# Attention output split over ten steps from step 48, and four rows of the output projection as filler

## The chip, the cores and the metric

The kernel runs on one core of a Trainium2 chip. The metric is the time of one execution on the device in microseconds; the kernel before took 1182.82 us (median of three runs, 1179.34 to 1183.29).

## The reference

A decoder trunk of two layers on one sequence of 1024 tokens with 1024 channels, in float32. The change is in the second layer only: forgetting attention with 16 heads of 64 channels, a gate, and the output projection.

```python
o = lax.map(one_block, (qb, fq, jnp.arange(nblk)))        # softmax(q k + forget bias) v, 8 blocks of 128 queries
o = o.transpose(1, 0, 3, 2, 4).reshape(bsz, L, ATTN_WIDTH)
o = o * jax.nn.silu(z.astype(jnp.float32))                # o_t in the kernel
return o.astype(h.dtype) @ w_out                          # rows f of the kernel
# and then x = x + gate * y
```

## The kernel before

All activations lie transposed: channels on the 128 partitions, tokens along the free side. A matrix of 1024 channels is eight tiles k = 0 to 7 of 128 x 1024, and most work goes by half of the tokens, i = 0 and 1 (512 each). A product in float32 is made from parts: `split` (line 100) writes a high part on ACT (L94) and the rest, x minus high part, on DVE (L102) or, for some weights, on POOL; `project_part` (L113) then issues three matmuls of 128 x 128 by 512 for each k. One half of a row of the output projection is thus 24 matmuls into one PSUM tile.

The attention runs as a list of 64 steps: heads 0 to 15, and for each head four blocks c = 0 to 3 of 256 queries, with 2c + 2 key blocks in block c. Step j first issues the scores of step j + 2 (`scores`: matmuls `sp`, DVE minimum `pr`/`mx`, ACT exponent, DVE reciprocal `sm`, POOL scaling of `pr`), then its own `values`: PE transposes `tp`, their split on ACT (`pth`) and DVE (`ptl`), matmuls `ov`, an ACT copy `ob` and a DVE sum `oc`. After each odd head (h = 1) and each odd block, POOL multiplies half i of tile p of `o_t` (which holds the gated z of two heads) by `oc` (L1301); this half is then done. For p = 6 and 7 it is split at once.

Filler is a generator from which the loop takes parts, each of three matmuls: two per step up to step 59, four from step 60 on, and all that is left behind step 63 (`some_fill`). A part is queued behind the last `ov` of its step on PE. First it gives the z projection (`zb`, eight strips of 16 parts); by the count of calls the last part of z on half 0 is given at step 47, the last on half 1 at step 51. Then comes `first_rows`. Before the change it makes tiles `aH`, `aL` for both halves, and begins rows of the output projection: row 0 over k = 0 to 5 for half 0, then half 1, each parked (evacuated with the residual into a tile `xr`); then rows 1 and 2 on half 0 over all k, and the rest of row 0 on half 0. The splits of the twelve halves of `o_t` that are done by then (`todo`) are asked for by this generator: three before its first part, one before each of the next nine. Where a part needs a half that isn't done, the call returns with nothing.

Behind the loop, the rest: row 1 on half 1 (in a PSUM bank of its own, around the wait for the last split), the rest of row 0, and rows 2 to 7, each half a tile `pj_f`, evacuated by DVE (`xr`, L1224) and stored.

The weights of a row come by one load into `w_raw` (a single buffer) and a split into `w_hi`, `w_lo` (two buffers each); row 2's go into a buffer `wf` that held the keys of head 14. The order of instructions on each engine is set by a planner at build time, from the order of the program, the dependences, its own estimate of durations, and the `issue_after` blocks, which put an instruction behind another one on its engine. Each engine, and each queue of loads, then runs in that order. PSUM tiles of z, of the rows f and of `ov` share two banks (`pj`).

Of the kernel before, what the change touches and what calls it, by code (L numbers as in the profile page):

```python
# [12 lines left out]
F32 = mybir.dt.float32  # L13
F32R = mybir.dt.float32r
# [6 lines left out]
P = 128  # L21
D = 1024
KT = D // P
# [8 lines left out]
HL = L // 2  # L32
# [2 lines left out]
MAGIC = 12582912.0  # L35
LOOK = 2
U_FIRST = 4
F_ROWS, Z_END = 3, 4
Z_FIRST, Z_STEP = 8, 2
ORDER = ((0, 0), (0, 1), (0, 2), (0, 3), (1, 0), (1, 1), (1, 2), (1, 3))  # L40
OUT_SEQ = ((0, 0), (1, 0), (0, 1), (1, 1), (2, 0), (2, 1), (3, 0), (3, 1),
# [4 lines left out]
def trunk(tc, a, out):  # L46
# [3 lines left out]
    with top:  # L50
# [24 lines left out]
        vec, at0 = {}, 0  # L75
# [29 lines left out]
        def act_tiles(more=0, halves=(0, 1)):  # L105
            return [[[apool.tile([P, HL + more * i], F32R, name=f"a{p}{k}_{i}", tag=f"a{p}{k}_{i}") if i in halves else None
                      for i in range(2)] for k in range(KT)] for p in "HL"]


        def project_part(ps, w, act, half, ks, k0=0, k1=KT - 1):  # L110
            for k in ks:
                for n, (wt, at) in enumerate(((0, 0), (0, 1), (1, 0))):
                    m = T.matmul(ps, w[wt][:, k, :], act[at][k][half], start=(k == k0 and n == 0), stop=(k == k1 and n == 2)).ins  # L113
            return m
# [91 lines left out]
        with l0:  # L206
# [141 lines left out]
            for k in (4, 5, 6, 7, 0, 1, 2, 3):  # L348
                pool, tag = ((s5, "ut"), (s5, "bbs"), (s5, "x1m"), (s5, "x2m"))[k - 4] if k >= 4 else (xp, "xw")
# [63 lines left out]
            for c in range(2):  # L413
                ps, m = chunk(w2, c, "u2")
# [377 lines left out]
            for k in range(KT):  # L792
                pool, tag = ((s5, "bb"), (s5, "bbs"), (s5, "x1m"), (s5, "x2m"), (sbm, "min_"), (s5, "ut"), (sb, "uu"), (sb, "uu"))[k]
# [22 lines left out]
        with l0b:  # L816
# [8 lines left out]
            for e, i in [(e, i) for e in range(KT - 2) for i in range(2)] + [(e, i) for i in range(2) for e in (KT - 2, KT - 1)]:  # L825
# [18 lines left out]
                if e:  # L844
                    ps = project(wg[e], act, i, f"g{e}_{i}", psa, "psa")
                    S.activation(sg, ps, AF.Sigmoid, bias=vec["b_glu"][:, e:e + 1])
                V.tensor_tensor(out=zs, in0=sg, in1=zs, op=ALU.mult)
                gated = V.tensor_tensor(out=part(yt[e], i), in0=part(yt[e], i), in1=jk(zs), op=ALU.mult).ins
# [7 lines left out]
            psb = top.enter_context(tc.tile_pool(name="psb", bufs=3, space=PSUM, side="right", reuse_waits="tile"))  # L856
            gate_a = mod_bias(16, 24, "gate_a")
            held, acc, seen, pending = {}, [None] * 2, [0, 0], None
            for e, i in OUT_SEQ:
# [6 lines left out]
                xr = wk.tile([P, HL], F32, name="xr", tag="zt2")  # L866
                xd = Q.dma_start(out=xr, in_=a["xT"][:, e, sl]).ins
                mod_load(xd)
                ps = project(held[e][1], act, i, f"o{e}_{i}", psa, "psa", pending)
# [35 lines left out]
        with l1a:  # L905
# [127 lines left out]
            for j, job in enumerate(("v0", "v2", "k0", "k2", "q0", "q2")):  # L1033
# [19 lines left out]
                for i in range(2):  # L1053
                    if job == "k2" and i:
                        act_b = act_tiles(0, (0,))
                    elif job == "q0" and i:
                        lx.close()
                        modx.close()
                        at0 = top.enter_context(tc.tile_pool(name="at0", bufs=2, side="right", reuse_waits="tile"))
# [150 lines left out]
            return scores(hds[n], c)  # L1210


        wf, parked, act2, done = {}, {}, [], set((k, 0) for k in range(KT - 2))

        def split_o(k, i):
            split(o_t[k][:, HL * i:HL * i + HL], act2[0][k][i], act2[1][k][i])

        def residual(e, i, park=False):
            xr = at_.tile([P, HL], F32, name="xr2", tag="park" if park else "oc", bufs=2 if park else 3)
            Q.dma_start(out=xr, in_=x1_d[P * e:P * e + P, HL * i:HL * i + HL])  # L1220
            return xr

        def gated(ps, e, xr):
            V.scalar_tensor_tensor(out=xr, in0=ps, scalar=gate_b[:, e:e + 1], in1=xr, op0=ALU.mult, op1=ALU.add)  # L1224

        def final(ps, e, i):
            xr = parked.pop((e, i)) if (e, i) in parked else residual(e, i)
            gated(ps, e, xr)
            Q.dma_start(out=out[P * e:P * e + P, HL * i:HL * i + HL], in_=xr)

        def f_tile(e, i, pool=None):
            return (pool or pj).tile([P, HL], F32, name=f"f{e}_{i}", tag="psb" if pool else "pj")

        def wf_(e):
            if e == 2 and e not in wf:

                w = at0.tile([P, 2, KT, P], F32R, name="wf2", tag="kk")
                raw = wpool.tile([P, KT, P], F32, name="w_raw", tag="w_raw", bufs=1)
                Q.dma_start(out=raw, in_=a["b_w_out"][e])
                wf[e] = w[:, 0], w[:, 1]  # L1240
                split(raw, *wf[e])
            elif e not in wf:
                wf[e] = weight_strip(a["b_w_out"][e], [P, KT, P], G if e < 2 else V)
            return wf[e]

        def first_rows():
            act2.extend(act_tiles())
            wf_(0), wf_(1)
            todo = [(k, i) for i in range(2) for k in range(KT - 2)]
            for i in range(2):  # L1250
                ps = f_tile(0, i)
                for k in range(KT - 2):
                    for _ in range(3 if (k, i) == (0, 0) else 1):
                        if todo:
                            with tc.issue_after(ends[-1][1]), tc.issue_after(ends[-1][2]):
                                split_o(*todo.pop(0))
                    project_part(ps, wf_(0), act2, i, (k,), 0, KT - 3)
                    yield
                parked[0, i] = residual(0, i, True)
                gated(ps, 0, parked[0, i])  # L1260
            wf_(2)
            for e in range(1, F_ROWS):
                ps = f_tile(e, 0)
                for k in range(KT):
                    while (k, 0) not in done:
                        yield
                    project_part(ps, wf_(e), act2, 0, (k,))
                    yield
                final(ps, e, 0)
                if e == 1:  # L1270
                    ps = f_tile(0, 0)
                    for k in (KT - 2, KT - 1):
                        project_part(ps, wf_(0), act2, 0, (k,), KT - 2)
                        yield
                    final(ps, 0, 0)

        fill = itertools.chain(z_fill, first_rows())

# [9 lines left out]
        ends = []  # L1288
        for j, (n, c) in enumerate(steps):
            if j + LOOK < len(steps):  # L1290
                pend.append(ahead(j + LOOK))
            if j < 2:
                with tc.issue_after(sp_end[-1]):
                    some_fill(3)
            ends.append(values(n, hds[n], c, pend.pop(0)))
            with tc.issue_after(ends[j][0]):
                some_fill(Z_STEP if j < 60 else Z_END)
            p, h = n // 2, n % 2
            if h and c % 2:
                sl = slice(HL * (c // 2), HL * (c // 2) + HL)  # L1300
                G.tensor_tensor(out=o_t[p][:, sl], in0=o_t[p][:, sl], in1=ocs.pop((p, c // 2)), op=ALU.mult)  # L1301
                done.add((p, c // 2))
                if p >= KT - 2:
                    split_o(p, c // 2)
        some_fill(999)

        psl = f_tile(1, 1, psb)
        project_part(psl, wf_(1), act2, 1, range(KT - 1))
        ps = f_tile(0, 1)
        project_part(ps, wf_(0), act2, 1, (KT - 2, KT - 1), KT - 2)  # L1310
        final(ps, 0, 1)
        project_part(psl, wf_(1), act2, 1, (KT - 1,))
        final(psl, 1, 1)
        for e in range(2, KT):
            for i in range(int(e < F_ROWS), 2):
                final(project(wf_(e), act2, i, f"f{e}_{i}"), e, i)

# [51 lines left out]
```

## Time and profile before

| | |
|---|---|
| median of three runs | 1182.82 us (1179.34 to 1183.29) |
| the profiled execution | 1183.26 us, of which the span from the first to the last instruction is 1181.1 us |
| PE busy | 97% of the span |
| DVE busy | 71% |
| ACT busy | 51% |
| POOL busy | 30% |
| mean granted clock of PE | 0.994 |

Times in views of the trace count from the span's start. A busy PE is not PE at its peak, since matmuls are pipelined and their ends modelled: matmuls of 512 columns issue every 0.23 us, and each record is some 0.4 us long, so records overlap. In the same way two DVE records in a row overlap a little at their edges. Idle time of an engine is put down to the semaphore that came last. A few matmul records are missing from the trace.

### The profile page before, as it was taken

To read this page: it belongs to the slowest core of one execution; us is meant where nothing else is said; L and a number is where in the kernel's file an instruction comes from. 1 tells how busy PE (TensorE), PEld (TensorE's weight loads), DVE (VectorE), ACT (ScalarE), POOL (GpSimd) and SP (SyncE) were. 2 spreads that over 40 slices of the span, in tenths; PEclk is the share of its full clock that TensorE was granted. 3 is DMA by queue.
4 is the path that set the end of the run, shared out by engine and by line. 5 is a ranking of instruction groups with operands and counts; after the bars stand their busy time and mean duration, and the time that the engine had idled before them with its cause. 6 is when DMAs were issued, how large, how long until landed. Compare 5 with 4: busy or idle time off the path is not lost.

```text
span 1181.1 us, 20618 instructions
## 1 busy us (share of the span) xinstructions
PE 1146.0 (97%) x7506; PEld 1018.0 (86%) x7506; DVE 838.3 (71%) x1721; ACT 605.6 (51%) x1141; POOL 349.8 (30%) x572
## 2 busy tenths in 40 slices
PE   8999999988999999999999999999999999989998
PEld 7688888887888887999999999988988889877786
DVE  6768999875788975836867654358888887897421
ACT  6665777565534333423222533247777777785210
POOL 2300122112000152211343354435545454544100
PEclk9999999999999999999999999999999999999999
DMA  9664567686875873258953438236647464541242
GB/s 360 205 182 141 150 171 178 151 198 180 316 248 188 291 277 99 81 195 261 309 177 108 167 102 251 90 109 143 133 102 161 105 147 102 132 90 45 98 162 71
DMA packets 94661, 197.11 MB, mean 167 GB/s; under 512 B 17728, under 2 KB 42496, under 8 KB 93024
## 3 DMA queue, kind: packets, MB, share of 16 engines
q1 hardware_dynamic: 86768, 174.17, 49.6%
q0 software_dynamic: 6048, 16.85, 4.7%
q10 hardware_dynamic: 1744, 4.77, 1.8%
q8 instruction: 59, 0.97, 0.3%
q14 instruction: 42, 0.34, 0.1%
HBM read 138.21 MB, written 46.27 MB: 156 GB/s over the span
## 4 chain that ended last, share of the span: by engine, by line
PE 73%; DVE 9%; ACT 7%; DMA 6%; issue 3%; POOL 1%; SPq 0%; ACTq 0%; DVEq 0%
PE tkps L940 22%; PE pj_g L113 8%; PE pj_o L113 7%; PE zb L113 6%; PE pj_f L113 5%; PE u L265 5%; PE tp L1184 4%; PE ov L1190 3%; DMA v<-v 3%; PE ov L1191 2%; PE sp L1151 2%; PE sp L1152 2%; PE f L113 2%; ACT pr L1159 1%; ACT w_hi L94 1%
## 5 line engine op out<-in xcount | busy, mean ns | idle before, releaser
L940 PE MATMUL tkps<-wvh,aH 128*128 128x256 f32 (+1 forms) x768 | 220.2, 287 | 3.3 <-DVE hnt L969 3.3
L940 PE MATMUL tkps<-wvl,aH 128*128 128x256 f32 (+1 forms) x768 | 216.6, 282 | 0.0
L940 PE MATMUL tkps<-wvh,aL 128*128 128x256 f32 (+1 forms) x768 | 216.0, 282 | 0.0
L940 PEld LDWEIGHTS tkps<-wvh,aH 128*128 128x128 f32 x768 | 145.2, 189 | 4.1 <-DVE hnt L969 3.7
L940 PEld LDWEIGHTS tkps<-wvl,aH 128*128 128x128 f32 x768 | 145.5, 189 | 0.3 <-issue 0.2
L940 PEld LDWEIGHTS tkps<-wvh,aL 128*128 128x128 f32 x768 | 144.8, 189 | 0.5 <-issue 0.5
L1161 POOL TENSOR_SCALAR pr<-pr,sm 128x128 f32<-128x128 f32 (+7 forms) x128 | 97.0, 763 | 98.5 <-DVE sm L1160 98.4
L1186 ACT ACTIVATE pth<-tp 128x512 fp32r<-128x512 f32 (+1 forms) x192 | 86.9, 489 | 57.0 <-PE ov L1190 30.8
L1159 ACT ACTIVATE pr<-pr,mx 128x128 f32<-128x128 f32 (+7 forms) x128 | 98.9, 773 | 27.1 <-DVE mx L1156 26.1
L1187 DVE TENSOR_TENSOR ptl<-tp,pth 128x512 fp32r<-128x512 f32 (+1 forms) x192 | 101.3, 552 | 11.2 <-ACT pth L1186 9.7
L1156 DVE CUSTOM_DVE_ANT_0 pr<-sp,msk 128x512 f32<-128x512 f32 (+3 forms) x128 | 72.8, 570 | 28.0 <-PE tp L1184 22.1
L713 POOL DMA_DIRECT2D y_d<-r x64 | 33.4, 552 | 200.2 <-ACT r L708 199.1
L94 ACT ACTIVATE w_hi<-w_raw 128x1024 fp32r<-128x1024 f32 x48 | 50.7, 1055 | 72.9 <-PE pj_f L113 28.1
L1184 PE MATMUL tp<-ident,pr 128*128 128x128 f32 x576 | 83.1, 273 | 3.0 <-DVE ptl L1187 2.7
L1190 PE MATMUL ov<-pth,vhl 128*128 128x256 f32 x320 | 84.5, 297 | 0.6 <-ACT pr L1159 0.4
L964 ACT ACTIVATE hsq<-tkps 128x256 f32<-128x256 f32 x64 | 24.3, 384 | 114.6 <-PE tkps L940 109.5
L1184 PEld LDWEIGHTS tp<-ident,pr 128*128 128x128 f32 x576 | 68.6, 140 | 13.8 <-DVE ptl L1187 4.7
L1191 PE MATMUL ov<-ptl,vhl 128*128 128x256 f32 x320 | 80.1, 284 | 0.0
L1151 PE MATMUL sp<-kk,qs 128*128 128x256 f32 (+2 forms) x192 | 70.1, 368 | 3.9 <-DVE mx L1156 3.9
L967 POOL TENSOR_TENSOR hms<-hms,nhalf 128x4 f32<-128x4 f32 x64 | 70.8, 1106 | 5.3
L1152 PE MATMUL sp<-kk,q 66*128 66x256 f32 (+2 forms) x192 | 65.6, 345 | 0.0
L265 PE MATMUL z<-aH,w_hi 128*128 128x258 f32 (+2 forms) x192 | 62.7, 327 | 1.4 <-ACT ez L405 1.4
(346 smaller groups left out, 3154.6 us busy)
## 6 DMA issues: line engine op xcount, KB each, us to landing
modw<-modw SPq DMA_DIRECT2D x48, 512.0 KB
wvr<-kvq_w SPq DMA_DIRECT2D x12, 1024.0 KB
w_raw<-a_w_in SPq DMA_DIRECT2D x16, 512.0 KB
v_d<-vt POOLq DMA_DIRECT2D x32, 256.0 KB, 4.3
kk<-k_d SPq DMA_DIRECT2D x16, 512.0 KB
vhl<-v_d SPq DMA_DIRECT2D x16, 512.0 KB
qs<-q_d SPq DMA_DIRECT2D x32, 256.0 KB
w_raw<-a_w_out SPq DMA_DIRECT2D x10, 512.0 KB
```

Source lines behind the costliest of these rows:

```text
L113: m = T.matmul(ps, w[wt][:, k, :], act[at][k][half], start=(k == k0 and n == 0), stop=(k == k1 and n == 2)).ins
L265: m = T.matmul(ps[:, 0:c1 - c0], w[wt][:, k, :], act[at][k][i][:, c0:c1], start=(k == 0 and n == 0), stop=(k == KT - 1 and n == 2)).ins
L940: T.matmul(ps[:, 0:nv], at, wt[:, k, 0:nv], start=(n == 0), stop=(n == 3 * KT - 1))
L1151: T.matmul(sp[:, 0:wm_], qsl, kk[:, 0, lo:lo + wm_], start=True, stop=False)
L1152: sp_end.append(T.matmul(sp[:, 0:wm_], q1_[:, P * i:P * i + P], kk[0:HD + 2, 1, lo:lo + wm_], start=False, stop=True).ins)
L1159: S.activation(pr[:, 0:nk], pr[:, 0:nk], AF.Exp, scale=-1.0, bias=mx, accum_out=sm)
L1161: G.tensor_scalar(out=pr[:, 0:nk], in0=pr[:, 0:nk], scalar1=sm, scalar2=0.0, op0=ALU.mult, op1=ALU.add)
L1184: T.transpose(out=tp[:, b, :], in_=prs[qi][:, P * (b0 + b):P * (b0 + b) + P], identity=ident)
L1186: S.activation(pth[:, 0:m, dst], tp[:, 0:m, :], AF.Copy)
L1187: V.tensor_tensor(out=ptl[:, 0:m, dst], in0=tp[:, 0:m, :], in1=pth[:, 0:m, dst].bitcast(F32), op=ALU.subtract)
L1190: T.matmul(ov, vhl[:, b, :], pth[:, b - b0, :], start=(b == 0), stop=False)
L1191: end = T.matmul(ov, vhl[:, b, :], ptl[:, b - b0, :], start=False, stop=(b == nb - 1)).ins
```

## The change

The twelve splits are no longer asked for by the filler. The loop itself asks for them behind `values` of its step, by a table: 2, 1, 2, 1 at steps 48 to 51 (half 0 of tiles 0 to 5) and one at each of steps 52 to 57 (half 1). The tiles `aH`, `aL` are made for half 0 at step 48 and for half 1 at step 52. The splits stay tied behind `ob` on ACT and `oc` on DVE of their step.

`first_rows` now parks rows 0 and 1, each in both halves, over k = 0 to 5 (four parked tiles, 24 parts); then it makes the rest (k = 6, 7) of rows 0 and 1 on half 0, and then rows 2 and 3 on half 0 over all k: 44 parts in all, 30 before. Row 2's weights are asked for behind the third parked half row, row 3's behind the end of row 1 on half 0, into buffers that held head 14's queries. Behind the loop, the half row that is spread around the last split is row 2's, and rows 0 and 1 are both ended there on half 1.

```diff
--- before.py
+++ after.py
@@ -35,7 +35,8 @@
 MAGIC = 12582912.0
 LOOK = 2
 U_FIRST = 4
-F_ROWS, Z_END = 3, 4
+F_ROWS, Z_END = 4, 4
+SPLIT_AT = {48: 2, 49: 1, 50: 2, 51: 1, 52: 1, 53: 1, 54: 1, 55: 1, 56: 1, 57: 1}
 Z_FIRST, Z_STEP = 8, 2
 ORDER = ((0, 0), (0, 1), (0, 2), (0, 3), (1, 0), (1, 1), (1, 2), (1, 3))
 OUT_SEQ = ((0, 0), (1, 0), (0, 1), (1, 1), (2, 0), (2, 1), (3, 0), (3, 1),
@@ -1210,13 +1211,15 @@
             return scores(hds[n], c)
 
 
-        wf, parked, act2, done = {}, {}, [], set((k, 0) for k in range(KT - 2))
+        wf, parked, done = {}, {}, set((k, 0) for k in range(KT - 2))
+        act2 = [[[None] * 2 for _ in range(KT)] for _ in range(2)]
+        todo = [(k, i) for i in range(2) for k in range(KT - 2)]
 
         def split_o(k, i):
             split(o_t[k][:, HL * i:HL * i + HL], act2[0][k][i], act2[1][k][i])
 
         def residual(e, i, park=False):
-            xr = at_.tile([P, HL], F32, name="xr2", tag="park" if park else "oc", bufs=2 if park else 3)
+            xr = at_.tile([P, HL], F32, name="xr2", tag="park" if park else "oc", bufs=4 if park else 3)
             Q.dma_start(out=xr, in_=x1_d[P * e:P * e + P, HL * i:HL * i + HL])
             return xr
 
@@ -1232,47 +1235,43 @@
             return (pool or pj).tile([P, HL], F32, name=f"f{e}_{i}", tag="psb" if pool else "pj")
 
         def wf_(e):
-            if e == 2 and e not in wf:
-
-                w = at0.tile([P, 2, KT, P], F32R, name="wf2", tag="kk")
+            if e in (2, 3) and e not in wf:
+
+                if e == 2:
+                    w = at0.tile([P, 2, KT, P], F32R, name="wf2", tag="kk")
+                    wf[e] = w[:, 0], w[:, 1]
+                else:
+                    wf[e] = at0.tile([P, KT, P], F32R, name="wf3h", tag="qs"), at0.tile([P, KT, P], F32R, name="wf3l", tag="q1_0", bufs=1)
                 raw = wpool.tile([P, KT, P], F32, name="w_raw", tag="w_raw", bufs=1)
                 Q.dma_start(out=raw, in_=a["b_w_out"][e])
-                wf[e] = w[:, 0], w[:, 1]
                 split(raw, *wf[e])
             elif e not in wf:
                 wf[e] = weight_strip(a["b_w_out"][e], [P, KT, P], G if e < 2 else V)
             return wf[e]
 
+
+
         def first_rows():
-            act2.extend(act_tiles())
             wf_(0), wf_(1)
-            todo = [(k, i) for i in range(2) for k in range(KT - 2)]
-            for i in range(2):
-                ps = f_tile(0, i)
+            for e, i in ((0, 0), (1, 0), (0, 1), (1, 1)):
+                ps = f_tile(e, i)
                 for k in range(KT - 2):
-                    for _ in range(3 if (k, i) == (0, 0) else 1):
-                        if todo:
-                            with tc.issue_after(ends[-1][1]), tc.issue_after(ends[-1][2]):
-                                split_o(*todo.pop(0))
-                    project_part(ps, wf_(0), act2, i, (k,), 0, KT - 3)
+                    project_part(ps, wf_(e), act2, i, (k,), 0, KT - 3)
                     yield
-                parked[0, i] = residual(0, i, True)
-                gated(ps, 0, parked[0, i])
-            wf_(2)
-            for e in range(1, F_ROWS):
-                ps = f_tile(e, 0)
-                for k in range(KT):
+                parked[e, i] = residual(e, i, True)
+                gated(ps, e, parked[e, i])
+                if (e, i) == (0, 1):
+                    wf_(2)
+            for e in range(F_ROWS):
+                ps, k0 = f_tile(e, 0), 0 if e > 1 else KT - 2
+                for k in range(k0, KT):
                     while (k, 0) not in done:
                         yield
-                    project_part(ps, wf_(e), act2, 0, (k,))
+                    project_part(ps, wf_(e), act2, 0, (k,), k0)
                     yield
                 final(ps, e, 0)
                 if e == 1:
-                    ps = f_tile(0, 0)
-                    for k in (KT - 2, KT - 1):
-                        project_part(ps, wf_(0), act2, 0, (k,), KT - 2)
-                        yield
-                    final(ps, 0, 0)
+                    wf_(3)
 
         fill = itertools.chain(z_fill, first_rows())
 
@@ -1293,6 +1292,14 @@
                 with tc.issue_after(sp_end[-1]):
                     some_fill(3)
             ends.append(values(n, hds[n], c, pend.pop(0)))
+            for _ in range(SPLIT_AT.get(j, 0)):
+                k, i = todo.pop(0)
+                if k == 0:
+                    for p_, x in enumerate(act_tiles(0, (i,))):
+                        for kk_ in range(KT):
+                            act2[p_][kk_][i] = x[kk_][i]
+                with tc.issue_after(ends[-1][1]), tc.issue_after(ends[-1][2]):
+                    split_o(k, i)
             with tc.issue_after(ends[j][0]):
                 some_fill(Z_STEP if j < 60 else Z_END)
             p, h = n // 2, n % 2
@@ -1304,14 +1311,16 @@
                     split_o(p, c // 2)
         some_fill(999)
 
-        psl = f_tile(1, 1, psb)
-        project_part(psl, wf_(1), act2, 1, range(KT - 1))
-        ps = f_tile(0, 1)
-        project_part(ps, wf_(0), act2, 1, (KT - 2, KT - 1), KT - 2)
-        final(ps, 0, 1)
-        project_part(psl, wf_(1), act2, 1, (KT - 1,))
-        final(psl, 1, 1)
-        for e in range(2, KT):
+
+        psl = f_tile(2, 1, psb)
+        project_part(psl, wf_(2), act2, 1, range(KT - 1))
+        for e in range(2):
+            ps = f_tile(e, 1)
+            project_part(ps, wf_(e), act2, 1, (KT - 2, KT - 1), KT - 2)
+            final(ps, e, 1)
+        project_part(psl, wf_(2), act2, 1, (KT - 1,))
+        final(psl, 2, 1)
+        for e in range(3, KT):
             for i in range(int(e < F_ROWS), 2):
                 final(project(wf_(e), act2, i, f"f{e}_{i}"), e, i)
 
```

## Rows read from the trace of the kernel before

**Rows 1.** The page of the profile: busy time of each engine (first part), and the shares of the chain that ended last, by engine (fourth part).

```profile
PE 1146.0 (97%) x7506; PEld 1018.0 (86%) x7506; DVE 838.3 (71%) x1721; ACT 605.6 (51%) x1141; POOL 349.8 (30%) x572
...
PE 73%; DVE 9%; ACT 7%; DMA 6%; issue 3%; POOL 1%; SPq 0%; ACTq 0%; DVEq 0%
```

**Rows 2.** Busy time of each engine in windows of four steps, each from the last `oc` of one head to the last `oc` of the next: steps 44 to 47, then S1 to S4. Columns: window, its length, busy us of each engine (instructions), granted clock of PE, share of the DMA engines, GB/s.

```profile
1003.68:1022.70 19.02, 18.83 (x123) 16.63 (x123) 15.79 (x49) 14.37 (x34) 10.61 (x19) 1.00 0.59 137
1022.70:1041.68 18.98, 18.98 (x129) 17.25 (x128) 15.16 (x50) 13.94 (x35) 8.82 (x18) 1.00 0.56 113
1041.68:1067.58 25.90, 21.03 (x120) 16.84 (x120) 23.96 (x62) 20.52 (x47) 12.32 (x17) 0.96 0.39 92
1067.58:1091.65 24.07, 24.03 (x141) 20.61 (x141) 17.60 (x49) 15.08 (x33) 9.02 (x20) 0.97 0.11 34
1091.65:1109.23 17.58, 15.96 (x102) 13.10 (x101) 9.40 (x18) 6.81 (x15) 2.93 (x6) 1.00 0.15 53
```

**Rows 3.** The same view in windows of 5 us, from the middle of S2 to the start of S3.

```profile
1050.00:1055.00 5.00, 5.00 (x33) 4.36 (x32) 4.94 (x13) 3.26 (x9) 2.11 (x2) 1.00 0.00 2
1055.00:1060.00 5.00, 4.01 (x22) 2.74 (x20) 4.93 (x11) 4.44 (x10) 1.68 (x4) 1.00 0.00 0
1060.00:1065.00 5.00, 2.16 (x14) 1.75 (x15) 4.91 (x11) 2.12 (x7) 2.24 (x3) 1.00 0.00 0
1065.00:1070.00 5.00, 5.00 (x20) 4.07 (x21) 3.68 (x14) 3.65 (x10) 3.36 (x7) 0.66 0.67 193
```

**Rows 4.** PE's instructions in order of time: two matmuls of the filler in the window at the lower clock, and a later one. Columns: start, length, what.

```profile
1067.36 0.63 PE L113 MATMUL f<-aL,w_hi 128*128 128x512 f32 x1
1067.78 0.63 PE L113 MATMUL f<-aH,w_lo 128*128 128x512 f32 x1
...
1072.31 0.40 PE L113 MATMUL f<-aH,w_lo 128*128 128x512 f32 x1
```

**Rows 5.** What PE waited for between 1039.6 and 1116, in total: us, times, the longest.

```profile
PE sp L1151 <- DVE mx L1156: 3.4, 3, 1.8
PE tp L1184 <- DVE ptl L1187: 1.9, 3, 0.8
...
PE f L113 <- DVE aL L102: 0.3, 1, 0.3
PE f L113 <- DVE oc L1197: 0.2, 1, 0.2
```

**Rows 6.** The chain that ended last, in order of time, pieces of S2.

```profile
1053.64 2.39 DVE aL L102 x2
...
1063.01 1.12 DVE wf L102
```

**Rows 7.** The same chain at its end.

```profile
1115.74 61.41 PE pj_f L113 x264
1177.18 0.75 DVE xr L1224
```

**Rows 8.** The splits: ACT's part (x16: min/median/max ns, first and last start), DVE's part (the same), DVE's busy time for `aL` alone in S2, the first two `aL` (merged), and POOL's next instruction behind them.

```profile
L94 ACT ACTIVATE aH<-o_t x16: 613/624/636, 1046.8 to 1111.1; 128x512 fp32r<-128x512 f32 x16
...
L102 DVE TENSOR_TENSOR aL<-o_t,aH x16: 679/690/1778, 1048.4 to 1111.7; 128x512 fp32r<-128x512 f32 x16
...
1041.68:1067.58 25.90, 2.59 (x7) 1.46 (x7) 7.04 (x9) 0.96 0.39 92
...
1048.45 1.29 DVE L102 TENSOR_TENSOR aL<-o_t,aH 128x512 fp32r<-128x512 f32 x2
...
1049.28 0.20 POOL L1178 MEMSET pth<- 128x128 f32 x1 [2.29 <-PE ov L1190]
```

**Rows 9.** DVE and POOL beside each other, in order of time: two `aL` around POOL's product `o_t` (merged), the same product later with no `aL` beside it, and POOL's scaling of 896 columns without and with DVE's `wf` (1062.93, rows 10) beside it.

```profile
1053.64 2.39 DVE L102 TENSOR_TENSOR aL<-o_t,aH 128x512 fp32r<-128x512 f32 x2
...
1053.69 1.79 POOL L1301 TENSOR_TENSOR o_t<-o_t,oc 128x512 f32<-128x512 f32 x1 [0.57 <-DVE oc L1197]
...
1069.76 1.28 POOL L1301 TENSOR_TENSOR o_t<-o_t,oc 128x512 f32<-128x512 f32 x1
...
1037.24 1.01 POOL L1161 TENSOR_SCALAR pr<-pr,sm 128x896 f32<-128x896 f32 x1 [2.00 <-DVE sm L1160]
...
1063.11 1.90 POOL L1161 TENSOR_SCALAR pr<-pr,sm 128x896 f32<-128x896 f32 x1 [1.53 <-DVE sm L1160]
```

**Rows 10.** An evacuation (DVE, S2); row 2's weights: issue of the load on SP, ACT's and DVE's half of the split; row 4's in the tail: issue, and ACT's half of the split, which waits for the load.

```profile
1059.21 0.74 DVE L1224 SCALAR_TENSOR_TENSOR xr<-f,gate_b,xr 128x512 f32<-128x512 f32 x1
...
1045.78 0.35 SPq L1239 DMA_DIRECT2D w_raw<-b_w_out  x1
...
1060.00 1.05 ACT L94 ACTIVATE wf<-w_raw 128x1024 fp32r<-128x1024 f32 x1
...
1062.93 1.20 DVE L102 TENSOR_TENSOR wf<-w_raw,wf 128x1024 fp32r<-128x1024 f32 x1
...
1117.89 0.34 SPq L86 DMA_DIRECT2D w_raw<-b_w_out  x1
...
1123.36 1.06 ACT L94 ACTIVATE w_hi<-w_raw 128x1024 fp32r<-128x1024 f32 x1 [7.22 <-DMA w_raw<-b_w_out]
```

**Rows 11.** The last `ov` of the attention on PE, and the last subtraction of a split on DVE.

```profile
1108.50 0.28 PE L1191 MATMUL ov<-ptl,vhl 128*128 128x256 f32 x1
...
1111.72 0.69 DVE L102 TENSOR_TENSOR aL<-o_t,aH 128x512 fp32r<-128x512 f32 x1 [2.07 <-ACT aH L94]
```

## The prediction

> **What bounds the kernel now.** I read the page first: PE is busy for 97% of the span and the chain that ended last is PE for 73% [rows 1]. So the time is PE's work plus the time in which PE stands still or runs on a lower clock; the change must be judged by those two. Then I cut the region of the change into windows of four attention steps (one head), from the end of one head's last `oc` to the next [rows 2]. I call them S1 (steps 48 to 51), S2 (52 to 55), S3 (56 to 59) and S4 (60 to 63). In the window ahead of S1 and in S1 PE is as good as always busy and a head costs 19.0 us. S2 has the same attention work and the same number of filler parts (output projection in place of z), yet it costs 25.90 us, and PE is busy for 21.03 of them. There DVE is the full engine: 23.96 of 25.90. The five-microsecond windows show it sharper [rows 3]: from 1050 to 1065 DVE is busy for 4.91 to 4.94 of each 5 us while PE falls to 2.16; behind that the granted clock is 0.66 in 1065 to 1070, so a part of that window ran at 1.2 GHz, and a 512-column matmul issues every 0.43 us there instead of every 0.23 [rows 4]. What PE waited for, asked for the whole stretch, is DVE: `mx` 3.4 us and `ptl` 1.9 us [rows 5]. The chain of waits names what DVE was doing in between: `aL` of the splits, and one `wf` [rows 6]. So twelve splits of the gated attention output, which the generator of the filler asks for as soon as it begins at step 52 (four there, two in each of the next four steps), overfill DVE for one head.
>
> Behind 1115.74 there are 264 projection matmuls in 61.41 us, 0.2326 us each, without a gap, and then one `xr` [rows 7]. The tail is pure PE work.
>
> **What PE loses before.** Idle: 25.90 - 21.03 = 4.87 in S2, 0.04 in S3, 17.58 - 15.96 = 1.62 in S4. Clock: 0.04 x 25.90 + 0.03 x 24.07 = 1.76. Together 8.29 us [rows 2]. That is all that a better order can give back, since the matmuls of the projection are the same before and after: 16 half rows of 24.
>
> **Part 1, the splits.** They are moved, not removed: six into S1 (2, 1, 2, 1), four into S2, two into S3. Each is one ACT copy of 0.62 us and one DVE subtraction [rows 8]. ACT in S1 would have 13.94 + 6 x 0.62 = 17.7 us of 19, so it still fits. For DVE the price of one subtraction is the open number. Two of them back to back, with POOL idle, took 1.29 us, 0.65 each; the nine in S2 keep DVE busy for 7.04 us, 0.78 each (their records overlap at the edges, so the mean record is a little longer); the longest took 1.78 [rows 8, 9]. I take 0.78, since these stood among the same attention work. S1: 15.16 + 6 x 0.78 = 19.84 us of DVE work. Where DVE was the bound, it was busy for 98.5% of a window [rows 3], so S1 would last 19.84 / 0.985 = 20.1 us, 1.2 more than now. S2: 23.96 less the nine subtractions (7.04) and less the `wf` one (1.20, which goes to step 60) is 15.72; five come back (four of the list, and the one for heads 12 and 13 that both kernels make at step 53): 15.72 + 3.90 = 19.62, or 19.9 us, 0.9 over the 19.0 that PE needs. So S1 and S2 lose 2.1 us in place of 4.87 idle, and the clock does not fall, since PE would stand still for some 5% of S1 and S2, and ahead of its fall it stood still for 2.84 of 5 us [rows 3]. At 0.65 the two lose 0.6 together; at 0.95 they lose 4.0.
>
> No transfer hangs on the splits. What is queued behind a moved one on ACT and DVE are `pth`, `ptl` and `mx` of the next steps, for which PE waits; that is the cost just counted. The tiles they write are free in time: by the count of the calls, z's last part on the first half is issued at step 47 and on the second half at step 51, so the first six splits (half 0, from step 48) and the last six (half 1, from step 52) wait for nothing new.
>
> **Part 2, the filler.** From step 52 the loop calls the filler 32 times. Before, there are 30 parts, and five calls (at steps 60 and 61) find nothing, because row 1 stands at its last part and waits for heads 14 and 15; so PE has little to put between the transposes and `ptl`, and S4 loses 1.62 us [rows 2, 5]. After, there are 44 parts, no call at steps 58 to 61 comes back empty (these are parked parts of rows 0 and 1, whose inputs exist), and twelve parts are left for behind the loop. The matmuls only change place: fewer in the tail, more in S4. I take it that half of 1.62 is won, 0.8; the bounds are nothing and all of it, as the rest of the waits there is for the last heads' own `aL` and `oc`, which nothing moves. Before, the last split ends at 1112.4, 3.6 us behind the last `ov` [rows 11]; the twelve parts (36 x 0.2326 = 8.4 us) and row 2's second half (21 x 0.2326 = 4.9 us) cover that.
>
> **Part 3, what is added.** Two more `xr` evacuations of 0.74 us on DVE [rows 10], two more residual loads: they fall into S3 and S4, where DVE is busy for 17.60 of 24.07 and 9.40 of 17.58 [rows 2], and cost nothing; without that cover 1.5 us. Row 3's weights now come into the loop, in buffers of head 14: a load and a split (ACT 1.05, DVE 1.20 [rows 10]), hidden in S4 in the same way. From the issue of such a load to its split took 5.5 us in the tail [rows 10], and on SP it stands behind the store of row 1; between it and row 3's first matmul stand row 2's parts and step 63. If it came late, PE would wait for at most 5.5 + 2.3 us; but `w_raw` is free as soon as row 2's split is done, and the load for row 2 was issued at 1045.8, 14 us ahead of its use [rows 10], so I count nothing.
>
> **Sum.** Lost before 8.29, lost after 2.1 + 0.8 = 2.9: 5.4 us won. The profiled execution took 1183.26 us; the median of three is 1182.82, so 0.44 less on that scale: 1182.82 - 5.4 = 1177.4 us.
>
> **A rule against it.** In S2 one `aL` began at the same time as POOL's product `o_t`: POOL's took 1.79 us instead of 1.28, the two `aL` together 2.39 instead of 1.29; and POOL's scaling of 896 columns took 1.90 us beside `wf` instead of 1.01 [rows 8, 9]. The Trainium skill, "SBUF — State Buffer", section "Who interferes with whom", says that a VectorE instruction with two SBUF inputs and a GpSimd instruction that reads SBUF exclude each other for the whole of the first one. The trace agrees with that. POOL is busy for 8.82 of S1's 18.98 us, so the moved subtractions go where POOL works as much as in S2 (12.32 of 25.90) [rows 2].
>
> **The rivals.**
> (a) POOL blocks the moved splits, and the kernel gets slower. If each took the 1.78 of the worst row, S1 would last (15.16 + 6 x 1.78) / 0.985 = 26.2 and S2 (15.72 + 5 x 1.78) / 0.985 = 25.0: 13.2 us lost, with 0.8 in S4 and one fall of the clock (1.8) 15.8, that is 7.5 more than before: 1190.3. It decides from a mean of 1.26 us a split on: (30.88 + 11 x 1.26) / 0.985 - 38.0 + 0.8 = 8.2. For it: POOL's share in S1. Against it: the mean of nine among the same work is 0.78. The rule of the skill alone says no number of collisions. Chance 0.07.
> (b) The starved stretch only moves. S1 had no slack on PE, and DVE and ACT are both filled to 93% or more; if `pth` and `ptl` come late by another 1 us, the clock falls once (1.8) and S4 gives nothing back (0.8), 3.6 of the 5.4 are gone: 1181.0. For it: the order on each engine is planned anew. Against it: six splits in 19 us, not nine in 26 with `wf` beside them. Chance 0.22.
> (c) DVE has room after all: splits at 0.65 lose 0.6 and S4 is filled wholly; 7.7 won, 1175.1. Chance 0.13.
> (d) The change doesn't do what it says: the splits are tied only to lie behind their step's `oc`, so the planner may still place them late, beside the filler. Then about 1182.8. Against it: before, they ran at once where they were asked for (the first at 1048.45, nine of them in S2 [rows 8]). Chance 0.03.
> The forecast itself, with splits between 0.70 and 0.85 us and S4 between none and all: 1175.7 to 1179.0. Chance 0.55.
>
> **How the numbers follow.** 0.3% is 3.5 us, about what a measurement can tell here. Faster than 1179.3 are nearly all of the forecast and (c): 0.66. Within 0.3%: (b), (d) and the forecast's edge: 0.27. Slower: (a), 0.07. The range leaves out (a), and the outer part of (b) and (c): 1174.8 to 1182.2.
>
> **What would show it.** Right: S2 near 20 us (cut at the same `oc`s) with PE idle below 1.5; S1 between 19.4 and 20.5 with DVE above 18.5 us; no window at 0.66 between 1020 and 1075; 216 matmuls of `pj_f` (264 less two half rows) without a gap at the end; a span near 1175.7. Wrong: S1 above 21.5 us, subtractions with a mean above 1 us, a gap ahead of row 3 or row 4 in the tail, or a lower clock in S1.

## The result, and the profile after

The changed kernel takes 1175.91 us (median of six runs, 1174.35 to 1178.82) against 1183.05 us (six runs, 1179.34 to 1186.14): ratio 0.9938, 95% interval 0.9923 to 0.9953, so 7.1 us or 0.6% faster. The forecast was 1177.4, the range 1174.8 to 1182.2. The profiled execution took 1175.35 us, of which the span is 1173.5.

To compare kernels without what happens earlier in an execution, I measure a *stretch*: from the start of step 47's `oc` to the end of PE's last projection matmul. Before, it begins at 1023.00 (the second window of [rows 2] begins 0.3 us ahead of it) and ends at 1115.74 + 61.41 = 1177.15 [rows 7]: 154.15 us. After, it is 147.31 us, from 1022.21 to 1169.52: 6.84 less. The spans of the two profiles differ by 7.6 us; the remaining 0.8 us lie ahead of step 47, where nothing was changed. In the ten profiles of the experiments that `oc` starts anywhere between 1019.87 and 1024.16, so differences of whole times below some 2 us say little. Each stretch comes from one profile, but it repeats well: two kernels below whose order differs only behind the loop (the change and e7) agree in it to 0.02 us.

The windows of [rows 2] again, for the kernel after, cut at its own `oc`s: S1 to S4 and the tail (all that comes behind the last `oc`). Columns as there.

```profile
1022.21:1041.33 19.12, 18.98 (x124) 16.81 (x124) 17.81 (x54) 15.82 (x37) 8.18 (x18) 1.00 0.56 112
1041.33:1063.06 21.73, 20.54 (x130) 17.24 (x129) 20.22 (x55) 18.18 (x40) 10.29 (x17) 1.00 0.39 87
1063.06:1086.28 23.22, 22.16 (x135) 19.22 (x133) 18.12 (x51) 16.14 (x38) 11.18 (x19) 1.00 0.24 76
1086.28:1105.11 18.83, 18.31 (x117) 16.02 (x116) 10.90 (x20) 6.93 (x15) 1.99 (x5) 1.00 0.12 42
1105.11:1169.52 64.41, 64.40 (x278) 51.67 (x276) 15.46 (x19) 4.88 (x5) 1.29 (x1) 1.00 0.36 119
```

S2 fell from 25.90 to 21.73 us and its idle PE time from 4.87 to 1.19. S1 costs 19.12 (18.68 before, cut at its `oc`s). The granted clock is whole in all five, where S2 and S3 had 0.96 and 0.97. A window cut at `oc`s, which DVE makes, doesn't always hold the same matmuls: S1 and S2 together have 254 records of them here and 247 before, so lengths of single windows are compared with care. S4 is longer, since more of the projection lies in it, and the tail is 3.5 us shorter (67.92 before).

The same windows for `aL` alone (columns: PE, PEld and DVE), S1 to S3. In them the subtractions took 0.67, 0.75 and 0.82 us each.

```profile
1022.21:1041.33 19.12, 3.16 (x8) 1.51 (x8) 3.35 (x5) 1.00 0.56 112
1041.33:1063.06 21.73, 3.16 (x8) 1.51 (x8) 3.76 (x5) 1.00 0.39 87
1063.06:1086.28 23.22, 5.49 (x14) 2.63 (x14) 3.28 (x4) 1.00 0.24 76
```

What is left of PE's waits in S3 and S4 (columns of [rows 5]), and then DVE's and PE's instructions in order of time around the longest waits of S2 and S3. In S2 the transposes begin 0.68 us late, behind a `ptl` that ran after the subtraction at 1057.04; row 2's weight split comes later, at 1060.18. In S3 row 3's weight split runs on DVE at 1070.91, and the transposes behind the next `ptl` begin 1.03 us late.

```profile
PE tp L1185 <- DVE ptl L1188: 1.0, 1, 1.0
PE f L114 <- DVE oc L1198: 0.5, 1, 0.5
```

```profile
1057.04 0.69 DVE L103 TENSOR_TENSOR aL<-o_t,aH 128x512 fp32r<-128x512 f32 x1
...
1058.47 0.41 PE L1185 MATMUL tp<-ident,pr 128*128 128x128 f32 x2 [0.68 <-DVE ptl L1188]
...
1060.18 1.22 DVE L103 TENSOR_TENSOR wf<-w_raw,wf 128x1024 fp32r<-128x1024 f32 x1
...
1063.52 1.16 DVE L103 TENSOR_TENSOR aL<-o_t,aH 128x512 fp32r<-128x512 f32 x1
...
1070.91 1.21 DVE L103 TENSOR_TENSOR wf3l<-w_raw,wf3h 128x1024 fp32r<-128x1024 f32 x1
...
1072.88 0.63 PE L1185 MATMUL tp<-ident,pr 128*128 128x128 f32 x4 [1.03 <-DVE ptl L1188]
```

The chain's end, which answers to [rows 7]: the leftover parts and rows 0 to 2, then 216 matmuls in 50.23 us, without a gap.

```profile
1104.66 14.63 PE f L114 x63
1119.29 50.23 PE pj_f L114 x216
1169.55 0.75 DVE xr L1227
```

### The profile page after: what moved, and what is told of

It reads as the page before. It is cut to its first block, busy times and chain, and to the rows that moved or that the text cites. A ratio compares the mean times of both kernels' runs of the same rounds, so it can differ in the third digit from the quotient of the medians.

```text
span 1173.5 us, 20611 instructions
## 1 busy us (share of the span) xinstructions
PE 1142.8 (97%) x7506; PEld 1016.8 (87%) x7506; DVE 838.1 (71%) x1723; ACT 605.7 (52%) x1141; POOL 347.1 (30%) x572
## 4 chain that ended last, share of the span: by engine, by line
PE 70%; DVE 12%; ACT 8%; DMA 5%; issue 3%; POOL 0%; SPq 0%; ACTq 0%; DVEq 0%
PE tkps L941 23%; PE pj_g L114 7%; PE zb L114 6%; PE pj_o L114 6%; PE pj_f L114 4%; PE tp L1185 4%; PE u L266 3%; PE ov L1191 3%; PE f L114 3%; PE ov L1192 2%; PE sp L1152 2%; PE sp L1153 2%; DMA v<-v 2%; ACT pr L1160 2%; DVE r L218 2%
## 5 line engine op out<-in xcount | busy, mean ns | idle before, releaser
L95 ACT ACTIVATE w_hi<-w_raw 128x1024 fp32r<-128x1024 f32 x47 | 49.6, 1055 | 64.8 <-PE pj_f L114 19.8
```

## The experiments

The theory at the start: S2 was lost to DVE, which the bunch of splits overfills, and most of the gain is theirs. The main rival: the longer filler keeps PE busy, and the splits matter little. All stretches below are read as above. A ratio is to runs of the kernel before that were made beside the experiment; their medians are 1183.05 (the change), 1184.06 (e1 to e4), 1183.27 (e5 to e8) and 1182.91 (e9, e10).

| kernel | median us | ratio to before, 95% | stretch | S1 | S2 | S3 | S4 | tail |
|---|---|---|---|---|---|---|---|---|
| before | 1183.05 | | 154.15 | 18.68 | 25.90 | 24.07 | 17.58 | 67.92 |
| the change | 1175.91 | 0.9938 (0.9923 to 0.9953) | 147.31 | 19.12 | 21.73 | 23.22 | 18.83 | 64.41 |
| e1 splits only | 1177.17 | 0.9945 (0.9925 to 0.9965) | 149.34 | 19.11 | 21.72 | 23.77 | 16.80 | 67.94 |
| e2 filler only | 1181.16 | 0.9983 (0.9968 to 0.9998) | 153.66 | 18.68 | 28.39 | 23.51 | 18.67 | 64.41 |
| e3 one per step | 1175.31 | 0.9921 (0.9902 to 0.9940) | 147.43 | 18.69 | 22.08 | 22.02 | 20.22 | 64.42 |
| e4 weights on POOL | 1174.55 | 0.9923 (0.9905 to 0.9941) | 145.80 | 19.11 | 20.60 | 22.85 | 18.82 | 64.42 |
| e5 two bunches | 1180.62 | 0.9982 (0.9967 to 0.9996) | 153.15 | 22.36 | 24.88 | 22.66 | 18.83 | 64.42 |
| e6 before, on POOL | 1180.92 | 0.9977 (0.9963 to 0.9991) | 153.40 | 18.68 | 25.36 | 24.48 | 16.96 | 67.92 |
| e7 without row 3 | 1174.44 | 0.9926 (0.9905 to 0.9947) | 147.29 | 19.11 | 21.73 | 23.23 | 18.82 | 64.40 |
| e8 e3 and e4 | 1173.86 | 0.9924 (0.9905 to 0.9942) | 145.53 | 18.68 | 21.06 | 21.15 | 20.22 | 64.42 |
| e9 copies alone | 1178.78 | 0.9965 (0.9949 to 0.9980) | 151.28 | 18.70 | 23.45 | 22.50 | 18.70 | 67.93 |
| e10 subtractions alone | 1181.64 | 0.9990 (0.9971 to 1.0009) | 154.60 | 18.68 | 25.69 | 24.73 | 17.58 | 67.92 |

**e1, the splits alone.** The kernel before with the table of splits and the tiles made at steps 48 and 52; `first_rows` is as before, without its `split_o`.

```diff
+SPLIT_AT = {48: 2, 49: 1, 50: 2, 51: 1, 52: 1, 53: 1, 54: 1, 55: 1, 56: 1, 57: 1}
-                        if todo:                          # in first_rows
...
-                                split_o(*todo.pop(0))
+            for _ in range(SPLIT_AT.get(j, 0)):           # in the loop, behind values
...
```

> The kernel before with the table of splits alone (2, 1, 2, 1 at steps 48 to 51, one at 52 to 57); the filler stays as before (row 0 parked, 30 parts, rows 1 and 2 on half 0). Theory (DVE's bunch of splits was the loss, the filler gives little): S2 falls from 25.9 to 21 to 22.5 us, no lower clock between 1020 and 1075, some 5 to 6.5 us faster than before (1176.5 to 1178), PE idle in S4 stays near 1.6 us. Rival (the longer filler is what keeps PE busy): at most 2 us faster, 1181 or above. Second rival (the fall of the clock is nearly all of it): about 2 us faster, with PE idle in S2 still 4 us or more.

Measured: the stretch 4.81 us shorter, S2 21.72, no lower clock. PE's idle time in S4 stays as it was: 16.80 - 15.18 = 1.62. The theory holds; neither rival does (PE is idle for 1.19 us in S2, not 4). S2 and S4 of e1, and PE's longest wait in S4; ahead of it PE has no part of the filler for more than 5 us:

```profile
1039.42:1061.14 21.72, 20.53 (x130) 17.25 (x129) 20.23 (x55) 18.19 (x40) 10.32 (x17) 1.00 0.37 87
...
1084.91:1101.71 16.80, 15.18 (x98) 12.54 (x97) 9.39 (x17) 6.81 (x15) 2.96 (x6) 1.00 0.16 55
...
1094.48 0.66 PE L1185 MATMUL tp<-ident,pr 128*128 128x128 f32 x4 [0.83 <-DVE ptl L1188]
```

**e2, the filler alone.** The changed kernel with the splits asked for by the filler again.

```diff
-            for _ in range(SPLIT_AT.get(j, 0)):
...
+                    for _ in range(3 if (e, i, k) == (0, 0, 0) else 1):
+                        if todo:
...
+                                split_o(*todo.pop(0))
```

> The changed kernel with its filler (44 parts, four parked half rows, row 3 on half 0), but the twelve splits asked for by the filler as before: three ahead of its first part and one ahead of each of the next nine. Theory: S2 is again 24.5 us or more with 4 us or more of PE idle and a lower clock behind it; within 0 to 2 us of before (1181 to 1183), the gain only from S4. Rival (the longer filler): 1176 to 1178.

Measured: 1181.16, as the theory had it; PE is idle for 3.90 us in S2, a little under the 4 it named. S3, S4 and the tail take 106.59 us, as in the change (106.46), against 109.57 before; but S2 takes 28.39. The 5-us windows show DVE full while PE starves, and the clock at its lower level (1.2 GHz) for one of them wholly, and for most of the next:

```profile
1040.33:1068.72 28.39, 24.49 (x127) 19.68 (x126) 25.15 (x62) 22.59 (x49) 13.68 (x21) 0.84 0.38 97
...
1060.00:1065.00 5.00, 3.22 (x13) 2.42 (x12) 4.97 (x14) 2.29 (x7) 2.31 (x3) 0.50 0.20 56
1065.00:1070.00 5.00, 5.00 (x19) 4.12 (x19) 2.93 (x9) 3.78 (x9) 2.97 (x6) 0.54 0.55 161
```

So the bunch with the longer filler beside it costs more than with the shorter one, and the two parts don't simply add: 4.81 (e1) and 0.49 (e2), and together 6.84.

**e7, no row 3 in the filler.** `F_ROWS = 3` in the changed kernel.

> The changed kernel with rows 0 to 2 on half 0 in the filler and not row 3 (36 parts in place of 44, four parked half rows kept; row 3's weights are still loaded early). 32 calls are made in the loop, so no call comes back empty. Theory (part 2 is worth 2.0 us because no call is empty, not because parts are left over): the stretch from step 47 to PE's end stays within 0.4 us of the change's 147.31. Rival (the surplus behind the loop, or row 3's place, gives part of it): 148 to 149.3.

Measured: 147.29, the change's stretch in each window within 0.02 us. Row 3's place is worth nothing. Part 2 wins 149.34 - 147.31 = 2.03 us, against e1; what e7 leaves of it is the four parked half rows, with which no call of the filler comes back empty. That it is the empty calls, and not another effect of the new order, is argued from e1's rows above; no run separates the two.

**e9 and e10, which half of a split does the harm.** Both are the kernel before with its bunch of twelve splits. In e9 the twelve subtractions on DVE are left out (the matmuls read the high part twice), in e10 the twelve copies on ACT (DVE writes a maximum of `o_t` with itself, and the matmuls read that twice); there are as many matmuls as before.

```diff
-            split(o_t[k][...], act2[0][k][i], act2[1][k][i])
+            act2[1][k][i] = act2[0][k][i]                                  # e9, k < 6
+            copy_on(S, act2[0][k][i], x)
+            act2[0][k][i] = act2[1][k][i]                                  # e10, k < 6
+            V.tensor_tensor(out=act2[1][k][i], in0=x, in1=x, op=ALU.max)
```

> The kernel before, bunch and filler as they were, but the twelve splits make only ACT's high part; the twelve subtractions are left out and the matmuls read the high part in place of the low one (as many matmuls as before). Theory A (DVE's subtractions are the harm): S2 falls to 20 to 22 us, the stretch from step 47 to PE's end to 148 to 150.5 (154.15 before). Theory B (ACT's copies in a row, ahead of pth, are the harm): S2 stays at 24 us or more, the stretch at 152.5 or more. Theory C (both hold it, each alone enough): S2 23.5 to 25.

> The kernel before, bunch and filler as they were, but the twelve splits make only DVE's part: one DVE instruction with the same two inputs' width from SBUF (a maximum of o_t with itself), and the twelve ACT copies are left out; the matmuls read DVE's result in place of both parts. Theory A (DVE's instructions are the harm): S2 stays at 24 us or more, the stretch from step 47 to PE's end at 152.5 or more. Theory B (ACT's copies are): S2 20 to 22 us, the stretch 148 to 150.5. Theory C (both, each alone enough): S2 23.5 to 25.

S2 of e9, then of e10 (last fence: what PE waited for in e10 between 1041 and 1070):

```profile
1042.86:1066.31 23.45, 21.36 (x125) 17.79 (x124) 18.21 (x53) 20.30 (x47) 11.72 (x19) 0.95 0.41 102
```

```profile
1040.10:1065.79 25.69, 20.71 (x118) 16.90 (x118) 23.91 (x58) 14.25 (x33) 10.90 (x18) 0.93 0.38 94
```

```profile
PE sp L1151 <- DVE mx L1156: 1.6, 2, 0.9
PE ov L1191 <- DVE ptl L1187: 1.5, 1, 1.5
```

With DVE's half alone S2 is as bad as with both (25.69, the stretch 154.60), and ACT has 11 us to spare in it: theory A for e10. With ACT's half alone S2 is 23.45, between A's 20 to 22 and B's 24, a hair below C's band, and the stretch is 151.28, again between A and B: none of the three fits. So DVE's half does the whole harm by itself; idle PE time is 4.98 us in S2 with the subtractions alone, 2.09 with the copies alone. What the copies cost isn't settled: e9's stretch is 1.94 us longer than e1's, but the clock fell twice in e9, the second time in S4 (0.91 over 18.70 us, 1.7 us by the prediction's way of counting), where none of the twelve copies lies. PE was idle for 1.06 us of 5 at worst in S2 there.

**e6, the kernel before with the twelve subtractions on POOL.** `split_o(*todo.pop(0), G)`: the rest of each split on POOL.

> The kernel before, bunch and filler as they were, with the subtractions of the twelve splits on POOL in place of DVE. Theory (S2 is lost to DVE's load): some 6 us less on DVE in S2; S2 falls to 20.5 to 23 us, the stretch from step 47 to PE's end to 148.5 to 151.5 (154.15 before, 149.34 with the splits alone moved). Rival (the bunch blocks the chain whoever subtracts, or POOL's scaling of pr queues behind twelve subtractions of 1.2 us each): S2 stays at 24.5 us or more, POOL busy for over 20 us in it, the stretch above 152.5.

Measured: the rival's numbers, but not by the way that it names. DVE has 4.1 us less in S2 (19.85) and is not full, yet S2 takes 25.36. Four subtractions of 1.27 us stand in a row on POOL at 1047.76, ahead of a scaling of `pr`; PE doesn't wait for them, it is busy for all of 1050 to 1060. It starves from 1060 to 1065, and the waits name DVE, not POOL. There the one subtraction that DVE still makes in S2 (it belongs to heads 12 and 13) lasts 2.11 us beside two of POOL's (rows at the end of this document), and row 2's weight split follows, with one short instruction for `pr` in between. Then the clock is at its lower level for 5 us. The lines are S2, POOL's row, windows of 5 us, PE's waits between 1045 and 1075, and the weight split:

```profile
1041.94:1067.30 25.36, 21.25 (x125) 17.77 (x124) 19.85 (x53) 20.30 (x47) 21.49 (x27) 0.93 0.38 93
...
1047.76 5.06 POOL L102 TENSOR_TENSOR aL<-o_t,aH 128x512 fp32r<-128x512 f32 x4 [0.51 <-ACT aH L94]
...
1050.00:1055.00 5.00, 5.00 (x34) 4.42 (x33) 2.76 (x9) 3.41 (x9) 5.00 (x7) 1.00 0.00 0
1055.00:1060.00 5.00, 5.00 (x34) 4.38 (x33) 4.41 (x11) 4.93 (x10) 5.00 (x8) 1.00 0.01 2
1060.00:1065.00 5.00, 1.92 (x9) 1.14 (x8) 5.00 (x10) 3.59 (x10) 2.59 (x4) 0.89 0.00 0
1065.00:1070.00 5.00, 5.00 (x17) 4.31 (x18) 1.09 (x6) 1.52 (x3) 4.36 (x7) 0.50 0.69 206
...
PE sp L1151 <- DVE mx L1156: 2.6, 3, 1.4
PE ov L1191 <- DVE ptl L1187: 1.1, 1, 1.1
...
1063.13 1.22 DVE L102 TENSOR_TENSOR wf<-w_raw,wf 128x1024 fp32r<-128x1024 f32 x1
```

**e5, two bunches of six in the changed kernel.** `SPLIT_AT = {48: 6, 52: 6}`.

> The changed kernel with the twelve splits as two bunches, six at step 48 and six at step 52, so each head has as many subtractions as in the change or two more (S1 6, S2 7 with the one that steps 53 and 55 ask for, S3 fewer), but not spread. Stretch meant: from the last oc of step 47 to the end of PE's last matmul, 154.15 us before, 147.31 in the change, 149.34 with the splits alone moved. Theory (the sum of DVE's work in a head decides, the place in it hardly): S1 19 to 19.8, S2 22 to 23.5, the stretch 147 to 149.5. Rival (the bunch as such is the harm: steps behind it wait, PE starves and its clock falls): S1 or S2 2 us longer than in the change and a lower clock, the stretch 150 or more.

Measured: the rival again, and the theory falls in this form. S1 has 1.0 us more of DVE work than in the change (18.82 and 17.81) and lasts 3.24 us longer, with a clock of 0.92. The rows show the stall: six copies on ACT ahead of `pth`, three subtractions on DVE ahead of `ptl`, PE's transposes 1.88 us late, and then matmuls at the lower clock (512 columns every 0.43 us).

```profile
1021.31:1043.67 22.36, 20.48 (x126) 18.16 (x126) 18.82 (x56) 16.69 (x40) 8.58 (x18) 0.92 0.44 93
...
1025.55 3.22 ACT L95 ACTIVATE aH<-o_t 128x512 fp32r<-128x512 f32 x6
1028.79 1.04 ACT L1187 ACTIVATE pth<-tp 128x512 fp32r<-128x512 f32 x3
...
1029.53 1.88 DVE L103 TENSOR_TENSOR aL<-o_t,aH 128x512 fp32r<-128x512 f32 x3
1031.34 0.88 DVE L1188 TENSOR_TENSOR ptl<-tp,pth 128x512 fp32r<-128x512 f32 x2
...
1032.16 1.06 PE L1185 MATMUL tp<-ident,pr 128*128 128x128 f32 x8 [1.88 <-DVE ptl L1188]
1032.98 0.63 PE L1152 MATMUL sp<-kk,qs 128*128 128x512 f32 x1
1033.41 0.63 PE L1153 MATMUL sp<-kk,q 66*128 66x512 f32 x1
```

The theory as it stands after this: the sum of DVE's work in a head isn't the whole price. A run of foreign instructions ahead of `pth`, `ptl` or `mx` costs PE time even where DVE isn't full over the head, and a stall can cost the clock besides. e6's stall, with DVE at 19.85 of 25.36 us, fits that. It doesn't put the sum aside. In the kernel before no run on DVE is longer than two subtractions or one and a weight split (1062.25 and 1062.93); but the chain that ended last is DVE's from 1045.20 to 1064.80, with 0.31 us of PE and the issue gaps between. There DVE's load itself is the bound. The ends of that piece:

```profile
1045.20 0.70 DVE ptl L1187
...
1064.13 0.66 DVE pr L1156
...
1064.86 0.44 PE sp L1151
```

**e3, one split per step; e4, row weights on POOL; e8, both.** In the changed kernel:

```diff
-SPLIT_AT = {48: 2, 49: 1, 50: 2, 51: 1, 52: 1, ...
+SPLIT_AT = {j: 1 for j in range(48, 60)}           # e3, e8
-                split(raw, *wf[e])
+                split(raw, *wf[e], None, G)        # e4, e8
```

> The changed kernel with one split at each of steps 48 to 59. Theory (what counts is how many subtractions fall into one head beside 15 us of other DVE work and row weights): S1 loses nothing (DVE near 16.8 us), S2 is as in the change (four splits, 21 to 22 us), S3 has one or two splits more; within 1 us of the change (1175 to 1177). Rival (the bunches of two at steps 48 and 50 cost): 1 to 2 us faster than the change.

> The changed kernel with the subtraction of row 2's and row 3's weight split on POOL (2.4 us there for 1024 columns) instead of DVE (1.2 us). Theory (DVE full from 1055 to 1075 is what is left of the loss, 2.2 us of PE idle in S2 and S3): 0.5 to 1.5 us faster than the change, 1174.5 to 1175.5, PE idle in S2 and S3 together below 1.5 us. Rival (POOL's scaling of pr, queued behind a subtraction of 2.4 us, takes DVE's place): the same as the change or up to 1 us slower, with transposes waiting for POOL.

> The changed kernel with one split at each of steps 48 to 59 and the subtractions of rows 2's and 3's weights on POOL. Theory (DVE's load in S2 and S3 is what is left): PE idle in S2 and S3 together below 1 us, the stretch from step 47 to PE's end 145 to 146 (145.80 with the weights alone on POOL), 1173.5 to 1175 in all. Rival (S3 takes up what S2 gives back): 146 to 147, no better than the change with the weights on POOL.

Measured: e3 has the change's stretch (147.43): S1 and S3 are shorter by 0.43 and 1.20, S2 and S4 longer by 0.35 and 1.39. e4 is 1.51 us shorter in the stretch, and the 1.06 us of idle PE in S3 go to nothing. S2 is 1.13 us shorter too, but only because some of its matmuls lie in S3 (122 records in S2 and 141 in S3, 130 and 135 in the change): its idle time stays at 1.19, and its longest wait at 0.7. So row 3's weight split on DVE did cost, and row 2's isn't shown to. POOL has room for 2.4 us, one at a time. e8 has a stretch of 145.53 and the best median, 1173.86, as its theory had it; but PE is idle for 1.31 us in its S2, not below 1, and again nothing is idle in S3. The intervals of e4 and e8 overlap the change's, so they are shown to beat it in the stretch only, not in whole times. S3 of e4 and of e8, both without idle PE:

```profile
1060.51:1083.36 22.85, 22.85 (x141) 20.18 (x141) 17.26 (x50) 16.89 (x39) 12.48 (x20) 1.00 0.24 81
```

```profile
1062.22:1083.37 21.15, 21.15 (x136) 19.00 (x135) 17.74 (x55) 17.76 (x41) 15.46 (x23) 1.00 0.29 86
```

## Why the prediction was right, step by step

**What bounds the kernel.** Right: the change is mostly worth what PE stood still or ran slowly for around S2, and DVE's half of the splits alone brings that about (e10). The clock stayed whole, as said.

**Part 1.** Forecast: 5.4 - 0.8 = 4.6 us; measured with the splits alone (e1): 4.81. That the two agree is in good part luck. The sum takes what PE needs in S2 as 25.90 - 4.87 - 1.04 = 20.0 us where it counts the loss before, and as 19.0 where it counts the loss after. By its own windows, S1 and S2 go from 44.88 to 40.0 and S3 wins 0.76, 5.6 in all. In e1, S1 and S2 won only 3.75 (44.58 to 40.83), and S3 to the tail 1.06 (109.57 to 108.51).

By windows, in the change: S1 was to last 20.1 us, 0.3 of them ahead of step 47's `oc`, and lasted 19.12. The five subtractions that fell into it took 0.67 us each, not 0.78, and the sixth fell behind step 51's `oc`, into S2. S2 was to last 19.9 and lasted 21.73: PE is busy for 20.54 of them, more than the 19.0 that a head was taken to need, and idle for 1.19. I took row 2's weight split (1.20 us) out of S2, since the program asks for it at step 60; the planner put it at 1060.18, in S2 as before. That is wrong in the sum of DVE's work, but it isn't what PE waited for: the long wait, 0.68 us, ended at 1058.47, and e4 has it too.

The pricing, the sum of DVE's work over 0.985, has the right cause for the kernel before, where DVE's chain has no break, but it is only a floor: it gives 24.3 us for S2 before (25.90 measured), 20.5 for S2 of the change (21.73), 19.1 for S1 of e5 (22.36) and 20.2 for S2 of e6 (25.36).

**Part 2.** The direction was right, the term mis-sized: 0.8 forecast, 2.03 measured (e1 to the change). I priced it by PE's idle time in S4, 1.62, and took half. In S3 and S4 the idle time is 0.46 + 1.62 in e1 and 1.06 + 0.52 in the change, only 0.5 less; the other 1.5 us lie in time that counts as busy: with the same matmuls (525 and 526 records) and a whole clock in both, PE is busy for 106.41 us in S3, S4 and the tail of e1 and for 104.87 in the change, so their records overlap less in e1. Stalls too short to show as idle time were closed, I take it by a filler that always has a part ready. The 2.03 is what is left after the wait behind row 3's weight split (1.03 us in S3), which e1 doesn't have.

**Part 3.** "I count nothing" was right for row 3's load and for the evacuations (no gap in the tail), wrong for row 3's weight split on DVE: it ran in S3, not hidden in S4, and PE waited 1.03 us behind it. With it and row 2's on POOL the stretch is 1.51 us shorter (e4).

**The rivals.** (a) did not come: the mean of a subtraction was 0.71 us over S1 and S2, far from the 1.26 from which the change would lose. POOL does delay one here and there, the longest took 1.16 us. It is delayed itself, too: its product `o_t` at 1050.83, begun beside the subtraction of 1050.78, took 1.8 us where [rows 9] has 1.28 alone, and the chain that ended last goes through it. (b) did not come in the change, but e5 shows that it was near: the same splits in two runs of six lose the clock and 5.8 us of the 6.84. (c) came near in time, by another way than its own: PE was idle for 1.33 us in S1 and S2, not for 0.6, and more than all of S4's idle time was won. (d) did not come.

**The sum.** 4.81 and 2.03 make the stretch's 6.84; 5.4 was forecast, short by part 2. Of the signs that were to show it right, these came: PE idle for 1.19 us in S2, no lower clock, 216 matmuls at the end without a gap. These didn't: S1 between 19.4 and 20.5 with DVE above 18.5 (19.12 and 17.81), and S2 near 20 (21.73).

## What to carry to other kernels

Side work for an engine that feeds the bound one has two prices: its sum, which is a floor, and the run that it forms ahead of the feeding instructions. Here moving twelve splits out of one head, spread by ones and twos, won 4.81 us, and in two runs of six most of the gain was gone (e5). To move the work to another engine is no way out by itself (e6). Keep filler long enough that it has a part wherever the bound engine would wait, and don't read its worth from idle time alone. Where a planner sets the order, a step is where the trace shows it, not where the program asks for it.

## What was not expected of the hardware

A fall of the granted clock came at milder stalls than the one of [rows 3]: in e9 PE was busy for 3.94 us of 1060 to 1065 and the clock was 0.89 there and 0.77 in the next 5 us; in the change PE was busy for 3.94 us of 1070 to 1075, and in e5 for 3.24 of 1050 to 1055, and the clock stayed whole. From these runs I can't say which stall costs it; that stays open. DVE and POOL do exclude each other, as rows of e6 show: the one subtraction that DVE makes there, at 1060.75, lasts until 1062.86, while POOL's two, begun at 1059.79, end at 1062.31. That is 2.11 us against 0.67 to 0.69 for most others, and PE starved behind it:

```profile
1059.79 2.52 POOL L102 TENSOR_TENSOR aL<-o_t,aH 128x512 fp32r<-128x512 f32 x2
...
1060.75 2.11 DVE L102 TENSOR_TENSOR aL<-o_t,aH 128x512 fp32r<-128x512 f32 x1
```

The Trainium skill, "SBUF — State Buffer", section "Who interferes with whom", has this as a lock that is held for a whole instruction; the rows agree. In the change it struck seldom: the mean subtraction in S1 and S2 was 0.71 us.
